# Six block copies per head batch, from ScalarE instructions to DMA transfers inside SBUF, in a chunked RWKV-7 and gated-MLP trunk

## The chip, the core and the metric

The kernel runs on one core of a Trainium2 chip (trn2). The metric is the device time of one launch in microseconds; lower is better. A core has TensorE (PE: matmuls, with weight loads shown apart as PEld), VectorE (DVE), ScalarE (ACT), GpSimd (POOL) and SyncE (SP), each with its own instruction queue worked off in order, and 16 DMA engines that carry out the transfers which SP and ACT issue.

## The reference, cut to what matters

The input is 256 tokens of width 2048 in float32. Layer 0 is a bidirectional RWKV-7 mixer of 64 heads of width 64, layer 1 a chunked gated MLP; a final norm closes it. Only layer 0 is touched here:

```
z = h @ w_in                              # 2048 -> r, k, v, gate of 4096 each, and low-rank columns
per head, in both directions, token by token:
  S_t = S_{t-1} diag(w_t) + (S_{t-1} a_t) b_t^T + v_t k_t^T ;   y_t = S_t r_t
out = (group_norm(y) + bonus) * silu(gate) @ w_out
```

The kernel does not step through tokens. It cuts the 256 tokens into 4 chunks of 64 and solves the inner dependence of a chunk with the inverse of a 64x64 unit triangular matrix, for each head, direction and chunk.

## The kernel before

**Batches.** Layer 0 is worked off in 16 batches of 4 heads (256 channels). A batch has 2 directions, 2 tiles of 128 channels, 4 chunks and 2 heads a tile, so 32 triangular matrices. Half h = 0 or 1 (a head of the tile) sits in partitions h*64 to h*64+63, and 16 matrices lie behind each other in the free dimension (index u). `plan` and the loop at the end of the mixer run several batches at once, each one step behind the next: in period p, `mains` projects k and r for batch p and v and gate for batch p-1, `before(p-1)` makes the gram matrices and their inverses, and `after(p-2)` runs the chunk chain. A batch takes about 77 us.

**The weight feed.** All projections are matmuls against weights that stream from HBM. `convert` loads a tile of 128x1024 values into `raw` (SP issues it, L145; L143 for the small low-rank weights `raw_wu`), ACT rounds it into `whi` (L150), DVE makes the rest `wlo` (L151), and PE takes three matmuls of 256 columns from each 128x128 block (L165, L166, L167). There are two `raw` buffers and three pairs of `whi`/`wlo`; a load waits for the `wlo` of the load two before it. A batch takes 16 such tiles (k, r, v, g: four each) and one `raw_wu`. After the last batch the feed turns to `raw_o`, the weights of the output projection.

**The inverse.** `grams` writes the masked gram matrices of a batch into Gs (DVE, L589). `inverses` inverts each 64x64 matrix by 32x32 blocks: the diagonal blocks go into Dt (four ACT copies, L623), DVE transposes Dt (La, L627), runs 62 small steps (L637, L639) and transposes the result into TD and Tn (L642, L643). The lower left block of Gs goes into NQ (L624). PE multiplies NQ with Tn into qp (L651), ACT copies that to the other rows of NQ (L653), PE multiplies with TD (L657), and ACT puts the product into TTs (L660) beside the two diagonal blocks taken from TD (L661, L662). TTs has one buffer for all batches.

**The chain.** For each of the 4 chunks `chain` runs xp (L713), Xs (ACT, L718), uu with TTs (L722), SUV (ACT, L724), then the next state sp (L729) and the outputs yp (L716, L731), and SUV again from the state (ACT, L741). `values` writes transposed v into SUV (ACT, L680) and issues four transfers inside SBUF on SP: two from AR into the part of Gs that `inverses` has read (Gs<-AR, L684), two into RC (RC<-AR, L684). The first pair waits until Dt and NQ have been read, the second until the previous batch's yp has read RC.

**What sets the order.** Each `yield` gives a due time inside the period, and the generators are drained by due time. From that stream the compiler's scheduler makes one fixed order for each engine; a kernel with other instructions gets another order everywhere in the mixer. An engine never passes an instruction that waits.

Of the kernel before, what the change touches and what calls it, by code (L numbers as in the profile page):

```python
# [22 lines left out]
def trunk(tc, x, norm_g, final_norm_g, w_in, mu_prev, mu_next, w0, w_up, a0, a_up, k_k, k_a, r_k,  # L23
          ln_w, ln_b, w_out, g_w_in, g_ln_g, g_ln_b, g_w_s, g_b_s, g_w_out, out):
    nc = tc.nc
    V, S, G, PE = nc.vector, nc.scalar, nc.gpsimd, nc.tensor
# [33 lines left out]
    def sm(name, tag="pg", bufs=2):  # L60
        return psm.tile([P, 512], F32, tag=tag, name=name, bufs=bufs)
# [280 lines left out]
    TTs = c2.tile([P, 2, 16, C], F32, name="TTs")  # L342
# [268 lines left out]
    def inverses(b, f):  # L611

        Gs, AR = f["Gs"], f["AR"]

        def lane(name):
            return se.tile([P, 16 * 33], F32, tag="ln", name=f"{name}{b}", bufs=3)

        Dt = lane("Dt")[:, :512].rearrange("p (t u) -> p t u", u=16)
        NQ = sc.tile([P, 16, 32], F32, tag="vy", name=f"NQ{b}", bufs=2)
        for h in range(2):  # L620
            for q in range(2):
                r0 = h * 64 + q * 32
                S.copy(Dt[r0:r0 + 32].rearrange("p t u -> p u t"), Gs[q * 32:q * 32 + 32, h, :, q * 32:q * 32 + 32])  # L623
            S.copy(NQ[h * 64:h * 64 + 32], Gs[0:32, h, :, 32:64])  # L624
        yield TSUB[0]
        La = se.tile([P, 32, 32], F32, tag="La", name=f"La{b}")
        V.transpose(La, Dt.unsqueeze(2).to_broadcast([P, 32, 2, 16]))  # L627
        xs = lane("X")
        G.memset(xs[:, :512], 0.0)
        G.tensor_scalar(xs.rearrange("p (m r) -> p m r", r=33)[:, :, 0:32:16], diag, 1.0, None, ALU.mult)  # L630
        X = xs[:, :512].rearrange("p (s t) -> p s t", t=16)
        TD = lane("TD")[:, :512]
        for j in range(31, 0, -1):
            yield TSUB[1] - (TSUB[1] - TSUB[0] - 2) * j / 31
            m, n = j // 2, 16 - j // 2
            tv = TD[:, :j * n].rearrange("p (s t) -> p s t", t=n)
            V.tensor_tensor(tv, La[:, j, 0:j].unsqueeze(2).to_broadcast([P, j, n]),  # L637
                            X[:, j:j + 1, m:].to_broadcast([P, j, n]), ALU.mult)
            V.tensor_tensor(X[:, 0:j, m:], X[:, 0:j, m:], tv, ALU.add)  # L639
        yield TSUB[1]  # L640
        Tn = lane("Tn")[:, :512]
        V.transpose(TD.rearrange("p (u t h) -> p t h u", t=16, h=2), X.rearrange("p s t -> p t s"))  # L642
        V.transpose(Tn, TD)  # L643
        TD, Tn = [t.rearrange("p (u t) -> p u t", t=32) for t in (TD, Tn)]
        qp = sm(f"qp{b}", "pq", 1).rearrange("p (u t) -> p u t", t=32)
        R0 = [slice(h * 64, h * 64 + 32) for h in range(2)]
        R1 = [slice(h * 64 + 32, h * 64 + 64) for h in range(2)]
        yield TQ[0]
        for u in range(16):
            for h in range(2):  # L650
                PE.matmul(qp[R1[h], u], NQ[R0[h], u], Tn[R0[h], u], start=True, stop=True)  # L651
        for h in range(2):
            S.copy(NQ[R1[h]], qp[R1[h]])  # L653
        yield TQ[1]
        for u in range(16):
            for h in range(2):
                PE.matmul(qp[R0[h], u], NQ[R1[h], u], TD[R1[h], u], start=True, stop=True)  # L657
        yield TQ[1] + 2
        for h in range(2):
            S.copy(TTs[R0[h], h, :, 32:64], qp[R0[h]])  # L660
            S.copy(TTs[R0[h], h, :, 0:32], TD[R0[h]])  # L661
            S.copy(TTs[R1[h], h, :, 32:64], TD[R1[h]])  # L662

    def values(b, f):

# [121 lines left out]
    def before(b, f):  # L787
        yield from grams(b, f, 1)
        yield from inverses(b, f)
# [340 lines left out]
    for tt in range(TT):  # L1130
        rstd2 = rms(total(part2[:, tt:tt + 1], f"ssq2_{tt}", hp), f"rstd2_{tt}", hp, V)
        for m in range(NM):
            h = h1[m][:, tt]
# [37 lines left out]
```

## Time and profile before

| what | value |
|---|---|
| median of 3 runs | 2230.92 us (2229.87 to 2234.58) |
| the profiled execution | 2229.16 us, span 2227.4 us |
| granted TensorE clock | 0.995 |
| busy: PE, PEld, DVE, ACT, POOL | 2179.0, 1944.7, 1608.1, 1345.2, 171.8 us |
| mixer batches, by their inverses | first Dt copy at 105.6 us, last at 1254.6 us |
| output projection with the feed alone | from about 1262 to 1445 us |
| gated MLP, its projections and the final norm | from about 1445 us on |

The busy time of an engine is the union of its instructions. A PE interval overlaps the next one, since matmuls are pipelined: in the rows of the timeline a 256-column matmul lasts 0.28 us but the next starts 0.12 us after it. A wait in the table of waits is idle time of an engine, put down to what ended last before it went on.

### The profile page before, as it was taken

To read this page: it belongs to the slowest core of one execution; us is meant where nothing else is said; L and a number is where in the kernel's file an instruction comes from. 1 tells how busy PE (TensorE), PEld (TensorE's weight loads), DVE (VectorE), ACT (ScalarE), POOL (GpSimd) and SP (SyncE) were. 2 spreads that over 40 slices of the span, in tenths; PEclk is the share of its full clock that TensorE was granted. 3 is DMA by queue.
4 is the path that set the end of the run, shared out by engine and by line. 5 is a ranking of instruction groups with operands and counts; after the bars stand their busy time and mean duration, and the time that the engine had idled before them with its cause. 6 is when DMAs were issued, how large, how long until landed. Compare 5 with 4: busy or idle time off the path is not lost.

```text
span 2227.4 us, 48630 instructions
## 1 busy us (share of the span) xinstructions
PE 2179.0 (98%) x19984; PEld 1944.7 (87%) x19984; DVE 1608.1 (72%) x3121; ACT 1345.2 (60%) x2128; POOL 171.8 (8%) x230
## 2 busy tenths in 40 slices
PE   7999999999999999999999999999999999999998
PEld 7889999999999999999999877778888888888886
DVE  5797788787977977887888764465546777777444
ACT  6556777777767676776767664464444444444443
POOL 2210110011001101100010000000000000000000
PEclk9999999999999999999999999999999999999999
DMA  5555444454445544444545555586766666665664
GB/s 167 140 145 142 109 126 134 125 137 112 130 127 143 139 126 131 129 125 136 137 124 138 167 174 177 173 263 189 221 204 190 198 189 195 195 193 192 195 198 154
DMA packets 352687, 356.01 MB, mean 160 GB/s; under 512 B 78160, under 2 KB 300112, under 8 KB 352336
## 3 DMA queue, kind: packets, MB, share of 16 engines
q1 hardware_dynamic: 332208, 331.66, 51.6%
q10 hardware_dynamic: 20256, 21.24, 3.2%
q8 instruction: 157, 2.57, 0.5%
q14 instruction: 66, 0.54, 0.1%
HBM read 329.78 MB, written 6.29 MB: 151 GB/s over the span
## 4 chain that ended last, share of the span: by engine, by line
PE 69%; ACT 10%; DMA 9%; DVE 8%; issue 3%; ACTq 0%; SPq 0%; POOL 0%; POOLq 0%; DVEq 0%
PE uacc L204 5%; PE gacc L204 5%; DMA raw_o<-in_rwkv_w_out_dram 3%; PE oacc L166 3%; PE oacc L167 3%; PE oacc L165 3%; PE gp L584 3%; PE gacc L206 3%; PE uacc L206 3%; PE vacc L167 3%; PE vacc L165 3%; PE vacc L166 3%; ACT Dt L623 2%; PE accv L165 2%; PE accg L167 2%
## 5 line engine op out<-in xcount | busy, mean ns | idle before, releaser
L204 PE MATMUL uacc<-z,whi_u 128*128 128x512 f32 x512 | 179.0, 394 | 0.0
L204 PE MATMUL gacc<-z,whi_g 128*128 128x512 f32 x512 | 177.3, 393 | 0.0
L167 PE MATMUL accg<-zh,wlo_wg 128*128 128x256 f32 x512 | 149.6, 292 | 2.5 <-DVE wlo_wg L151 2.4
L165 PE MATMUL accv<-zh,whi_wv 128*128 128x256 f32 x512 | 149.2, 291 | 1.1 <-ACT whi_wv L150 1.1
L167 PE MATMUL accr<-zh,wlo_wr 128*128 128x256 f32 x512 | 148.7, 290 | 0.6 <-DVE wlo_wr L151 0.5
L165 PE MATMUL acck<-zh,whi_wk 128*128 128x256 f32 x512 | 148.1, 289 | 1.1 <-ACT whi_wk L150 1.1
L165 PE MATMUL accr<-zh,whi_wr 128*128 128x256 f32 x512 | 149.0, 291 | 0.0
L165 PE MATMUL accg<-zh,whi_wg 128*128 128x256 f32 x512 | 148.4, 290 | 0.0
L166 PE MATMUL accr<-zl,whi_wr 128*128 128x256 f32 x512 | 148.1, 289 | 0.0
L167 PE MATMUL accv<-zh,wlo_wv 128*128 128x256 f32 x512 | 147.5, 288 | 0.1
L167 PE MATMUL acck<-zh,wlo_wk 128*128 128x256 f32 x512 | 146.2, 286 | 1.0 <-DVE wlo_wk L151 1.0
L166 PE MATMUL accv<-zl,whi_wv 128*128 128x256 f32 x512 | 147.2, 287 | 0.0
L166 PE MATMUL accg<-zl,whi_wg 128*128 128x256 f32 x512 | 147.0, 287 | 0.0
L166 PE MATMUL acck<-zl,whi_wk 128*128 128x256 f32 x512 | 147.0, 287 | 0.0
L206 PE MATMUL uacc<-z,wlo_u 128*128 128x256 f32 x512 | 142.4, 284 | 0.0
L206 PE MATMUL gacc<-z,wlo_g 128*128 128x256 f32 x512 | 140.2, 279 | 0.0
L151 DVE TENSOR_TENSOR wlo_v<-raw_v,whi_v 128x1024 fp32r<-128x1024 f32 x64 | 78.4, 1225 | 80.4 <-ACT whi_v L150 80.4
L151 DVE TENSOR_TENSOR wlo_o<-raw_o,whi_o 128x1024 fp32r<-128x1024 f32 x64 | 78.2, 1224 | 77.5 <-ACT whi_o L150 77.2
L639 DVE TENSOR_TENSOR X<-X,TD 128x126 f32<-128x126 f32 (+22 forms) x496 | 126.5, 255 | 9.4
L637 DVE TENSOR_TENSOR TD<-La,X 128x126 f32<-128x126 f32 (+22 forms) x496 | 125.6, 253 | 10.6
L151 DVE TENSOR_TENSOR wlo_p<-raw_p,whi_p 128x1024 fp32r<-128x1024 f32 x60 | 73.9, 1232 | 75.7 <-ACT whi_p L150 75.7
L150 ACT CAST whi_p<-raw_p 128x1024 fp32r<-128x1024 f32 x60 | 63.1, 1051 | 91.5 <-PE oacc L167 87.3
(331 smaller groups left out, 6842.3 us busy)
## 6 DMA issues: line engine op xcount, KB each, us to landing
raw_wk<-in_rwkv_w_in_dram SPq DMA_DIRECT2D x64, 512.0 KB, 3.7
raw_wr<-in_rwkv_w_in_dram SPq DMA_DIRECT2D x64, 512.0 KB, 3.7
raw_wv<-in_rwkv_w_in_dram SPq DMA_DIRECT2D x64, 512.0 KB, 3.7
raw_wg<-in_rwkv_w_in_dram SPq DMA_DIRECT2D x64, 512.0 KB, 3.7
raw_o<-in_rwkv_w_out_dram SPq DMA_DIRECT2D x64, 512.0 KB, 4.0
raw_v<-in_gmlp_w_in_dram SPq DMA_DIRECT2D x64, 512.0 KB, 3.7
raw_u<-in_gmlp_w_in_dram SPq DMA_DIRECT2D x64, 512.0 KB, 3.5
raw_g<-in_gmlp_w_in_dram SPq DMA_DIRECT2D x64, 512.0 KB, 3.6
```

What stands on the lines that cost most here:

```text
L150: latest[0] = S.copy(hi, raw)
L151: latest[1] = V.tensor_tensor(lo, raw, hi.bitcast(F32), ALU.subtract)
L165: PE.matmul(acc, a[0], b[0], start=first, stop=False, skip_group_check=True)
L166: PE.matmul(acc, a[0], b[1], start=False, stop=False, skip_group_check=True)
L167: PE.matmul(acc, a[1], b[0], start=False, stop=last, skip_group_check=True)
L204: PE.matmul(acc.rearrange("p h t -> p (h t)"), hi[:, j, cs], zc[:, k].rearrange("p h t -> p (h t)"), start=k == 0, stop=False, skip_group_ ...
L206: PE.matmul(acc[:, 0], lo[:, j, cs], zc[:, k, 0], start=False, stop=k == KT - 1, skip_group_check=True)
L584: PE.matmul(gp[h][:, c].rearrange("p q t -> p (q t)"), BK[H[h], d, cl, c].rearrange("p q t -> p (q t)"), AR[H[h], d, cl, c].rearrange("p q ...
L623: S.copy(Dt[r0:r0 + 32].rearrange("p t u -> p u t"), Gs[q * 32:q * 32 + 32, h, :, q * 32:q * 32 + 32])
L637: V.tensor_tensor(tv, La[:, j, 0:j].unsqueeze(2).to_broadcast([P, j, n]), X[:, j:j + 1, m:].to_broadcast([P, j, n]), ALU.mult)
L639: V.tensor_tensor(X[:, 0:j, m:], X[:, 0:j, m:], tv, ALU.add)
```

## The change

Three of the four kinds of block copies in `inverses` leave ACT. The copy of the lower left block of Gs into NQ (two a batch) and those of the diagonal blocks of TD into TTs (four a batch) become DMA transfers that SP issues. Each moves 32 partitions x 16 x 32 values, 64 KB in runs of 128 bytes. The TTs transfers are also written earlier in the source, ahead of the due time `TQ[1] + 2`. The Dt copies and those out of PSUM (L653, L660) stay on ACT. Lines behind the first edit keep their numbers up to L657; then the new transfers are L659 and L660, and old lines from L658 stand one higher from there on (L684 becomes L685, L722 becomes L723), the copy of qp into TTs becomes L663.

```diff
@@ inverses
             for q in range(2):
                 r0 = h * 64 + q * 32
                 S.copy(Dt[r0:r0 + 32].rearrange("p t u -> p u t"), Gs[q * 32:q * 32 + 32, h, :, q * 32:q * 32 + 32])
-            S.copy(NQ[h * 64:h * 64 + 32], Gs[0:32, h, :, 32:64])
+            nc.sync.dma_start(NQ[h * 64:h * 64 + 32], Gs[0:32, h, :, 32:64])
...
         for u in range(16):
             for h in range(2):
                 PE.matmul(qp[R0[h], u], NQ[R1[h], u], TD[R1[h], u], start=True, stop=True)
+        for h in range(2):
+            nc.sync.dma_start(TTs[R0[h], h, :, 0:32], TD[R0[h]])
+            nc.sync.dma_start(TTs[R1[h], h, :, 32:64], TD[R1[h]])
         yield TQ[1] + 2
         for h in range(2):
             S.copy(TTs[R0[h], h, :, 32:64], qp[R0[h]])
-            S.copy(TTs[R0[h], h, :, 0:32], TD[R0[h]])
-            S.copy(TTs[R1[h], h, :, 32:64], TD[R1[h]])
```

The order moves in three places that matter below; a digit behind a name is the batch. First SP's queue where batch 9's gram matrices are done (about 782 to 795 us before). Before:

```order
L145 DMA raw_wr10_0_10767<-in_rwkv_w_in_dram 128x4x256
L145 DMA raw_wr10_4_10826<-in_rwkv_w_in_dram 128x4x256
L145 DMA raw_wr10_8_10904<-in_rwkv_w_in_dram 128x4x256
L684 DMA Gs9_10428<-AR9_10072 64x16x64 x2
L145 DMA raw_wr10_12_10965<-in_rwkv_w_in_dram 128x4x256
```

SP's queue at the same place now:

```order
L145 DMA raw_wr10_0_10767<-in_rwkv_w_in_dram 128x4x256
L145 DMA raw_wr10_4_10826<-in_rwkv_w_in_dram 128x4x256
L624 DMA NQ9_10742<-Gs9_10428 32x16x32 x2
L685 DMA Gs9_10428<-AR9_10072 64x16x64 x2
L145 DMA raw_wr10_8_10904<-in_rwkv_w_in_dram 128x4x256
L145 DMA raw_wr10_12_10965<-in_rwkv_w_in_dram 128x4x256
```

The load `raw_wr10_8` has moved from ahead of the transfers inside SBUF to behind them. The Gs transfers overwrite what the NQ transfers read, so they wait for these to land. Then ACT's queue at the same place. Before:

```order
L150 CAST whi_wk10_12_10702<-raw_wk10_12_10700 128x1024
L680 COPY SUV8_10606<-vp8_10608 64x4x128 x4
L150 CAST whi_wr10_0_10769<-raw_wr10_0_10767 128x1024
L623 COPY Dt9_10741<-Gs9_10428 32x16x32 x2
L624 COPY NQ9_10742<-Gs9_10428 32x512
L623 COPY Dt9_10741<-Gs9_10428 32x16x32 x2
L624 COPY NQ9_10742<-Gs9_10428 32x512
L718 COPY Xs8_0_10680<-xp8_0_10671 128x256
L150 CAST whi_wr10_4_10828<-raw_wr10_4_10826 128x1024
```

ACT's queue there now:

```order
L719 COPY Xs8_0_10680<-xp8_0_10671 128x256
L150 CAST whi_wk10_12_10702<-raw_wk10_12_10700 128x1024
L725 COPY SUV8_10606<-uu8_0_10718 64x4x64 x2
L623 COPY Dt9_10741<-Gs9_10428 32x16x32 x4
L150 CAST whi_wr10_0_10769<-raw_wr10_0_10767 128x1024
L742 COPY SUV8_10606<-SJ8_0_10796 64x4x64 x2
L150 CAST whi_wr10_4_10828<-raw_wr10_4_10826 128x1024
```

The four Dt copies now stand together with the NQ copies gone, and the first chunk of batch 8's chain (Xs, SUV) has moved ahead of them. Last, SP's queue where TTs of batch 8 is filled (about 751 to 762 us before). Before:

```order
L145 DMA raw_wg8_0_10229<-in_rwkv_w_in_dram 128x4x256
L684 DMA RC_333<-AR8_8968 64x16x64 x2
L145 DMA raw_wg8_4_10289<-in_rwkv_w_in_dram 128x4x256
L145 DMA raw_wg8_8_10373<-in_rwkv_w_in_dram 128x4x256
L145 DMA raw_wg8_12_10457<-in_rwkv_w_in_dram 128x4x256
```

And now:

```order
L685 DMA RC_333<-AR8_8968 64x16x64
L145 DMA raw_wg8_0_10229<-in_rwkv_w_in_dram 128x4x256
L685 DMA RC_333<-AR8_8968 64x16x64
L145 DMA raw_wg8_4_10289<-in_rwkv_w_in_dram 128x4x256
L145 DMA raw_wg8_8_10373<-in_rwkv_w_in_dram 128x4x256
L659 DMA TTs_331<-TD8_9662 32x16x32
L660 DMA TTs_331<-TD8_9662 32x16x32
L659 DMA TTs_331<-TD8_9662 32x16x32
L660 DMA TTs_331<-TD8_9662 32x16x32
L145 DMA raw_wg8_12_10457<-in_rwkv_w_in_dram 128x4x256
```

The four TTs transfers stand ahead of the load `raw_wg8_12`. They wait for batch 8's TD (L642), which DVE's order places right behind the `wlo` of `wg8_0` now and right ahead of that of `wg8_12` before:

```order
L151 TENSOR_TENSOR wlo_wg8_0_10232<-raw_wg8_0_10229,whi_wg8_0_10231 128x1024
L755 BN_STATS st6_7_10302<-yp7_9559 128x6 x3
L642 STREAM_TRANSPOSE TD8_9662<-X8_9659 128x32x16
L755 BN_STATS st6_7_10302<-yp7_9559 128x6
L756 BN_AGGR mv7_10303<-st6_7_10302 128x2
```

The 62 small steps of the inverse have thus moved forward by about three weight tiles against the feed.

## The prediction, made before the changed kernel had run

> **What bounds the kernel now.** I read the page's busy times first, then the windows by stage, then the waits of PE, then the timeline around one batch's inverse.
>
> ```profile
> span 2227.4 us, 48630 instructions
> PE 2179.0 (98%) x19984; PEld 1944.7 (87%) x19984; DVE 1608.1 (72%) x3121; ACT 1345.2 (60%) x2128; POOL 171.8 (8%) x230
> ...
> 80.00:240.00 160.00, 150.47 (x1618) 142.25 (x1617) 131.13 (x271) 98.79 (x155) 22.21 (x25) 0.96 0.51 137
> 240.00:880.00 640.00, 636.61 (x7823) 590.60 (x7822) 525.93 (x1238) 460.81 (x800) 69.34 (x85) 1.00 0.48 128
> 880.00:1262.00 382.00, 377.04 (x4679) 353.04 (x4678) 317.65 (x745) 275.63 (x476) 34.78 (x49) 1.00 0.50 134
> 1262.00:1445.00 183.00, 177.44 (x1405) 139.74 (x1405) 97.94 (x176) 91.18 (x140) 4.96 (x5) 0.99 0.55 175
> ```
>
> The columns of a window are busy us of PE, PEld, DVE, ACT and POOL, then clock, DMA share and GB/s. In the mixer PE is the bound: it idles 160.00 - 150.47 = 9.5 us while the first batches fill, 3.4 us in the eight batches from 240 to 880 us, 5.0 us from there to 1262, and 5.6 us in the output projection, 23.5 us together. ACT, the engine that the change relieves, is busy 460.81 of 640 us. So most of what ACT saves is not on the path. What can be won is idle time of PE that ends on ACT, and what PE's own new order is worth. The idle time of PE from 80 to 1310 us, the rows that carry the argument:
>
> ```profile
> PE yp L731 <- ACT SUV L724: 2.8, 4, 1.1
> PE accg L167 <- DVE wlo_wg L151: 2.4, 1, 2.4
> ...
> PE vp L673 <- ACT TTs L660: 1.3, 2, 0.9
> ...
> PE accv L165 <- ACT whi_wv L150: 1.1, 1, 1.1
> PE qp L657 <- ACT NQ L653: 1.1, 1, 1.1
> ...
> PE xp L713 <- ACT SUV L680: 0.7, 3, 0.3
> PE accr L167 <- DVE wlo_wr L151: 0.5, 1, 0.5
> ```
>
> Each row has total us, times, longest. The two rows on wlo say that PE has hardly ever waited for a projection weight: once for a gate tile, once for an r tile, in all 16 batches. The feed runs ahead of PE.
>
> **Part 1, what leaves ACT.** The copies, with minimum, median and maximum ns:
>
> ```profile
> L624 ACT COPY NQ<-Gs x32: 615/618/622, 107.8 to 1255.7; 32x512 f32<-32x512 f32 x32
> ...
> L661 ACT COPY TTs<-TD x32: 602/617/622, 171.9 to 1301.2; 32x512 f32<-32x512 f32 x32
> L662 ACT COPY TTs<-TD x32: 613/616/624, 172.5 to 1301.8; 32x512 f32<-32x512 f32 x32
> ```
>
> 96 copies of about 0.617 us are 59.2 us, 3.7 us a batch, and ACT should fall from 1345 to about 1286 us. Beside the 77 us that a batch takes nearly all of that is hidden already. On the path lie the places where a chain copy that PE waits for stands behind the removed ones in ACT's queue. One of them:
>
> ```profile
> 1023.64 2.18 ACT L623 COPY Dt<-Gs 32x512 f32<-32x512 f32 x2
> 1025.85 0.62 ACT L624 COPY NQ<-Gs 32x512 f32<-32x512 f32 x1
> 1026.48 0.76 ACT L724 COPY SUV<-uu 64x256 f32<-64x256 f32 x2
> ...
> 1026.90 0.33 PE L731 MATMUL yp<-SUV,Gs 128*64 128x64 f32 x2 [1.00 <-ACT SUV L724]
> ```
>
> PE lost 1.00 us waiting for a SUV copy that stood behind two NQ copies, 1.24 us. The five rows of waits on ACT above (SUV twice, TTs, whi_wv, NQ) add up to 7.0 us, and all but about 0.4 us of them begin within about seven us of removed copies. I credit **-6.6 us**. Bounds: 0, if the new order puts other instructions there, and -13 us as an estimate, about twice these rows, if the remaining small waits of PE on ACT go too.
>
> **Part 2, PE's new order.** PE executes the same matmuls. Counted in the two orders, it passes from one kind of work to another (weights, grams, chain, inverse) 3222 times before and 3163 times now. What such a passage costs is in the timeline:
>
> ```profile
> 701.07 0.28 PE L166 MATMUL acck<-zl,whi_wk 128*128 128x256 f32 x1
> 701.19 0.28 PE L167 MATMUL acck<-zh,wlo_wk 128*128 128x256 f32 x1
> 701.40 0.49 PE L584 MATMUL gp<-AR,BK 64*128 64x128 f32 x4
> ...
> 703.65 0.39 PE L165 MATMUL acck<-zh,whi_wk 128*128 128x256 f32 x1
> 703.88 0.28 PE L166 MATMUL acck<-zl,whi_wk 128*128 128x256 f32 x1
> ```
>
> A weight matmul follows another after 0.12 us; the step into the gram takes 0.21 us and the first one behind it 0.23 us, so about 0.1 us is lost at each passage. 59 passages less are **-5 us**, with ends of 0 (kinds differ in price) and -6.
>
> **Part 3, what SP and the DMA engines get.** Each batch adds six issues and 6 x 512 runs of 128 bytes. The trace has no such transfer. The nearest rows are the transfers inside SBUF that are there, in runs of 256 bytes, beside a weight load:
>
> ```profile
> raw_wr<-in_rwkv_w_in_dram SPq DMA_DIRECT2D x64, 512.0 KB, 3.7
> RC<-AR SPq DMA_DIRECT2D x32, 256.0 KB, 5.2
> Gs<-AR SPq DMA_DIRECT2D x32, 256.0 KB, 3.7
> ...
> L684 SPq DMA_DIRECT2D Gs<-AR x32: 590/596/665, 108.5 to 1256.3; - x32
> ...
> DMA to landing us min/median/max: 3.4/4.1/7.5
> ```
>
> An issue of 1024 runs costs SP 0.60 us; one of 512 runs should cost between that of a weight load, 0.37 us (below), and 0.60, so six cost 2.2 to 3.6 us of SP's 77. SP mostly waits. A landing takes 3.4 to 7.5 us; I take 3.7, since the pieces are smaller.
>
> Where can that reach PE? At batch 9 the load of wr10_8 now stands behind two NQ and two Gs transfers. Before:
>
> ```profile
> 783.95 1.29 DVE L589 TENSOR_TENSOR Gs<-gp,gmask 128x512 f32<-128x512 f32 x2 [1.57 <-PE gp L584]
> 787.59 0.37 SPq L145 DMA_DIRECT2D raw_wr<-in_rwkv_w_in_dram  x1
> 789.07 3.43 SPq L684 DMA_DIRECT2D Gs<-AR  x2
> 792.17 2.00 ACT L150 CAST whi_wr<-raw_wr 128x1024 fp32r<-128x1024 f32 x2
> 794.74 1.21 DVE L151 TENSOR_TENSOR wlo_wr<-raw_wr,whi_wr 128x1024 fp32r<-128x1024 f32 x1
> 800.15 0.28 PE L167 MATMUL accr<-zh,wlo_wr 128*128 128x256 f32 x1
> ```
>
> The load was issued at 787.59 and landed at about 791.3; its cast, the second of the two, began about 793.1, its wlo ended at 795.95, and PE used that first at 800.15. So its cover is 1.8 us ahead of the cast and 4.2 us behind wlo, 6.0 us. Now NQ can be issued when Gs is done, 785.24, twice 0.4 us; it lands by 789.7. The second Gs transfer waits for the fourth Dt copy, at about 786.2 + 4 x 1.09 = 790.6, and is issued by 791.2, then the load: 3.7 us later than before. Queueing behind small runs may add 1.5 us, which is what RC's 5.2 us stands above Gs's 3.7. That is 5.2 of 6.0 us: covered, with little left. Gs itself frees no later, since the wait for two NQ copies in ACT's queue is replaced by a landing that runs beside the Dt copies. At TTs four issues, 1.6 us, and their runs, up to about 2.8 us as an estimate (twice the 1.5 us above, rounded down), stand ahead of one gate tile a batch. TD is not late there: DVE makes it three tiles earlier than before, and the previous batch's uu must only have read TTs, which RC's transfer two places ahead needs of yp as well. I cost part 3 at **+2.5 us**: about 2 us in the output projection, where the last TTs transfers stand in a feed that is itself the bound (PEld is busy only 139.74 of 183 us there), and 0.5 us for the first batches, whose tiles come just in time. Ends: 0 and +27 us (below).
>
> **The sum.** 2229.2 us (the profiled execution; span 2227.4) - 6.6 - 5 + 2.5 = 2220.1 us. The median of the runs lies 1.8 us above that execution, so **2222 us**. Here 0.2%, 4.5 us, is about what a measurement can tell from no change.
>
> **Rival A: hidden, no change.** What ACT gives up is replaced by other waits of the same size. For it: PE idles only 3.4 us in eight batches, and the five rows come from a few chance meetings in the queues. Against it: the copies were really ahead of what PE waited for. Time: the median, about 2230 us, give or take 4.
>
> **Rival B: slower, the feed comes late behind the SBUF transfers.** 13 of the 16 batches have both Gs transfers between NQ and the next weight load. The load leaves SP at 785.24 + 0.8 + landing + 0.6 once that is later than 791.2; with the 1.5 us of queueing the cover of 6.0 us is used up at a landing of 5.4 us, and from there each further us is lost by PE. At 7.5 us, the largest of the rows, that is 2.1 us in each of 13 batches, +27 us; midway, 1.05 us and +14 us: 2230.9 + 14 = **2245 us**. For it: the runs are half as long as the 256-byte ones, whose 256 KB already take as long as 512 KB of weights. The Trainium skill points the same way: its page "DMA: Bandwidth & Descriptors", section "Issuing engines are not separate DMA queues", says that transfers of all issuers share the 16 DMA engines and interleave, and its section "Specifications" sets 512 bytes as the least run for full rate. By that section the longer landing would be the rule. The same page's section "Why small descriptors are slow (HBM only)" says the opposite for transfers inside SBUF, and by it this rival falls away. The trace sides with the first for 256-byte runs, which move half the bytes a microsecond of a weight load, and shows no 128. Against it: the DMA share there is 0.48, and PE waited for wlo twice in all.
>
> **Rival C: the chain gains more.** The new order has the inverse three tiles earlier and the chain's first copies ahead of Dt, so PE's later small waits go as well: -13 - 6 + 1 = -18, 2213 us. For it: 5.0 us of idle time from 880 to 1262 us. Against it: DVE, busy 525.93 of 640 us, sets these places too.
>
> **Chances.** My forecast (2217 to 2226) 0.42, rival C (2207 to 2217) 0.13, rival A 0.25, rival B 0.20. Faster by over 0.2%: forecast and C without their edges, 0.53; within 0.2%: 0.27; slower: 0.20. The range takes the forecast, A and most of C, and the mild end of B: 2209 to 2240.
>
> **What would show it.** ACT busy near 1286 us and 96 copies fewer; the wait of yp on SUV below 1 us in total; no new row of PE on wlo_wr or wlo_wg above 1 us; NQ landings of 3 to 4.5 us; SP's Gs<-AR waits on ACT Dt, not on NQ. It is wrong if PE waits on wlo_wr in many batches, if SP stands at TTs until TD is done, or if the PE waits on ACT only change places.

## The result, and the profile after

The changed kernel takes 2212.7 us (2208.5 to 2216.2, 4 runs) against 2232.5 us before beside it: ratio 0.991, 95% interval 0.989 to 0.994, about 20 us faster. The profiled execution took 2209.9 us. Its page, first the span and the busy times:

```profile
span 2208.1 us, 48735 instructions
PE 2169.0 (98%) x19984; PEld 1938.5 (88%) x19984; DVE 1611.7 (73%) x3121; ACT 1289.0 (58%) x2032; POOL 160.7 (7%) x230
```

ACT has 96 instructions and 56.2 us less. The span fell by 19.3 us: PE's idle time (span less busy) from 48.4 to 39.1 us, its busy time from 2179.0 to 2169.0. The same 19984 matmuls therefore take 10.0 us less even where PE does not wait. By stage (busy us of PE, PEld, DVE, ACT and POOL, then clock, DMA share, GB/s; the third stage ends, and the fourth begins, 12 us earlier than in the table of before):

```profile
80.00:240.00 160.00, 155.07 (x1638) 147.91 (x1637) 133.79 (x263) 95.26 (x149) 23.15 (x26) 0.95 0.53 140
240.00:880.00 640.00, 636.43 (x7953) 591.48 (x7952) 534.74 (x1275) 432.48 (x755) 64.08 (x86) 1.00 0.52 136
880.00:1250.00 370.00, 367.77 (x4627) 344.50 (x4626) 311.20 (x722) 256.15 (x441) 29.79 (x49) 1.00 0.55 143
1250.00:1430.00 180.00, 176.48 (x1336) 139.14 (x1335) 99.12 (x173) 89.34 (x134) 5.38 (x5) 1.00 0.59 181
```

From 240 to 880 us PE is as busy as before (636.4 and 636.6), but gets through 7953 matmuls instead of 7823. The waits of PE from 80 to 1310 us, the largest first:

```profile
PE accg L167 <- DVE wlo_wg L151: 2.8, 2, 2.4
PE gp L584 <- DVE Gs L589: 1.7, 1, 1.7
PE yp L732 <- ACT SUV L725: 1.4, 2, 0.8
PE xp L714 <- ACT SUV L681: 1.3, 1, 1.3
PE qp L657 <- ACT NQ L653: 0.9, 1, 0.9
PE oacc L165 <- ACT whi_o L150: 0.8, 2, 0.6
PE vp L674 <- ACT TTs L663: 0.7, 1, 0.7
...
PE uu L723 <- DMA Gs<-AR: 0.5, 1, 0.5
```

All rows of this view, with those left out here, sum to 11.9 us, against 21.1 us before. No r tile was waited for, and the new transfers show up at most in the 0.5 us of uu on Gs<-AR, which stands behind the NQ transfers in SP's queue.

Where the time went is seen at one place in the timeline, batch 12's gram matrices and batch 11's chain. After:

```profile
1004.40 0.69 PE L723 MATMUL uu<-Xs,TTs 128*64 128x64 f32 x16
1005.13 0.74 ACT L725 COPY SUV<-uu 64x256 f32<-64x256 f32 x2 [1.08 <-PE uu L723]
1006.21 1.29 DVE L589 TENSOR_TENSOR Gs<-gp,gmask 128x512 f32<-128x512 f32 x2 [0.90 <-PE gp L584]
1006.93 1.26 SPq L624 DMA_DIRECT2D NQ<-Gs  x2
1006.93 4.33 ACT L623 COPY Dt<-Gs 32x512 f32<-32x512 f32 x4 [1.06 <-DVE Gs L589]
1008.45 0.69 PE L730 MATMUL sp<-SUV,BT 128*64 128x64 f32 x16
1008.96 0.64 PE L732 MATMUL yp<-SUV,Gs 128*64 128x64 f32 x16
1010.12 1.80 SPq L685 DMA_DIRECT2D Gs<-AR  x2
```

Before, the rows that stand ahead of those shown in part 1:

```profile
1019.99 0.69 PE L722 MATMUL uu<-Xs,TTs 128*64 128x64 f32 x16
1020.79 2.20 ACT L623 COPY Dt<-Gs 32x512 f32<-32x512 f32 x2
1023.00 0.62 ACT L624 COPY NQ<-Gs 32x512 f32<-32x512 f32 x1
...
1023.65 3.44 SPq L684 DMA_DIRECT2D Gs<-AR  x2
```

In both, uu is done when Dt begins. Before, its copy into SUV had to wait for all six copies and started 5.7 us after the first of them; now it stands ahead of Dt and starts 1.8 us before it. The next two steps, sp and yp, then run while ACT does Dt, each in one block of 16. Before, PE lost 1.00 us in front of yp and began it with a piece of two. The groups of the chain's output in the table by line (count | busy us, mean ns | idle), before and after:

```profile
L731 PE MATMUL yp<-SUV,Gs 128*64 128x64 f32 x1024 | 59.4, 226 | 2.9 <-ACT SUV L724 2.8
L716 PE MATMUL yp<-SUV,RC 128*64 128x64 f32 x768 | 41.5, 222 | 0.0
```

```profile
L732 PE MATMUL yp<-SUV,Gs 128*64 128x64 f32 x1024 | 53.6, 225 | 1.4 <-ACT SUV L725 1.4
L717 PE MATMUL yp<-SUV,RC 128*64 128x64 f32 x768 | 37.2, 222 | 0.0
```

One matmul lasts as long as ever, but more of them overlap. Counted from start to start and without the waits, so that nothing counts twice, the steps of yp took 76.3 us before and 70.4 after. Of the unbroken groups of yp, 20 ran as one block of 16 before, and 49 do now.

That place is not one of its kind. Over batches 1 to 15, the SUV copy of the previous batch's first chunk starts ahead of Dt in 2 batches before, and in 9 after. In batches 9 to 15 it starts 8.2 us behind the first Dt copy before, and from then on 5.7 and some 16 us behind it in turn; after, from batch 8 on, 1.8 to 2.0 us ahead of it in every one. The gain follows that: the first matmul on v weights of batch 5 starts at 496.3 us before and 497.1 after, that of batch 14 at 1200.1 and 1185.6, so 1.7 us a batch (15.3 us over nine). The output projection and what is left of the last chains give the rest, and from the gated MLP on (1495.3 and 1475.5 us) the distance stays the same to within 0.5 us.

### The profile page after: what moved, and what is told of

Same layout as the page of the kernel before. It is cut to its first block, busy times and chain, and to the rows that moved or that the text cites. A ratio compares the mean times of both kernels' runs of the same rounds, so it can differ in the third digit from the quotient of the medians.

```text
span 2208.1 us, 48735 instructions
## 1 busy us (share of the span) xinstructions
PE 2169.0 (98%) x19984; PEld 1938.5 (88%) x19984; DVE 1611.7 (73%) x3121; ACT 1289.0 (58%) x2032; POOL 160.7 (7%) x230
## 4 chain that ended last, share of the span: by engine, by line
PE 77%; DMA 8%; DVE 7%; ACT 6%; issue 2%; POOL 0%; SPq 0%; ACTq 0%; POOLq 0%; DVEq 0%
PE uacc L204 5%; PE gacc L204 5%; DMA raw_o<-in_rwkv_w_out_dram 3%; PE gp L584 3%; PE oacc L166 3%; PE oacc L167 3%; PE oacc L165 3%; PE uacc L206 3%; PE gacc L206 3%; PE vacc L165 3%; PE vacc L166 3%; PE vacc L167 3%; PE accg L167 2%; PE accv L167 2%; PE accv L165 2%; PE accv L166 2%
```

## The experiments

Theory P: what counts is ACT's time at one place, between Gs and the chain's copies and casts, and of the removed copies only those of NQ stood there. Its main rival is O, that every kernel gets another order, which alone is worth some us either way. T and D belong to single runs. These are the letters from run 5 on. The first four expectations were written before P had this form: their R is wider, relief wherever PE waits on ACT, and gave each half of the change about 9 us.

All runs in one table: time, ratio to the kernel before measured beside it, batches out of 15 in which that first SUV copy starts ahead of Dt, PE's idle time (span less busy) and granted clock of the profiled execution. The kernel before runs at 2229 to 2233 us beside them, with 2 batches, 48.4 us idle, clock 0.995. Where a few us matter, runs that were not measured beside each other are compared below by their distance from it.

| kernel | us | ratio, 95% interval | SUV ahead | PE idle | clock |
|---|---|---|---|---|---|
| the change | 2212.7 | 0.991 (0.989 to 0.994) | 9 | 39.1 | 0.994 |
| 1 NQ alone by DMA | 2211.3 | 0.992 (0.990 to 0.993) | 10 | 42.2 | 0.996 |
| 2 TTs alone by DMA | 2228.5 | 0.999 (0.998 to 1.000) | 2 | 49.7 | 0.997 |
| 3 the change and six idle ACT copies | 2220.7 | 0.996 (0.994 to 0.997) | 8 | 42.8 | 0.995 |
| 4 TTs copies earlier, on ACT | 2229.8 | 1.000 (0.999 to 1.001) | 2 | 45.9 | 0.994 |
| 5 NQ by DMA and idle ACT copies in its place | 2222.6 | 0.997 (0.996 to 0.998) | 0 | 51.8 | 0.994 |
| 6 NQ alone by GpSimd | 2210.8 | 0.991 (0.990 to 0.993) | 10 | 37.8 | 0.995 |
| 7 before, another due time | 2234.7 | 1.002 (1.001 to 1.003) | 2 | 50.7 | 0.996 |
| 8 the change, another due time | 2209.0 | 0.990 (0.989 to 0.992) | 9 | 42.4 | 0.996 |
| 9 before, NQ copied twice | 2238.6 | 1.004 (1.003 to 1.006) | 0 | 50.6 | 0.991 |
| 10 NQ by DMA, Dt by GpSimd | 2231.4 | 1.001 (1.000 to 1.002) | 0 | 44.2 | 0.991 |
| 11 NQ by DMA, half of Dt by GpSimd | 2220.2 | 0.996 (0.994 to 0.997) | 2 | 41.3 | 0.994 |
| 12 all six copies by GpSimd | 2222.6 | 0.996 (0.994 to 0.997) | 7 | 42.1 | 0.992 |

**Each half alone.** Run 1 is the first edit alone:

```diff
-            S.copy(NQ[h * 64:h * 64 + 32], Gs[0:32, h, :, 32:64])
+            nc.sync.dma_start(NQ[h * 64:h * 64 + 32], Gs[0:32, h, :, 32:64])
```

> Only the NQ copies (two a batch) go by DMA; the four TTs copies stay on ACT as before. Theory R (relief: what counts is ACT time taken away ahead of what PE waits for): NQ stands right behind Dt in ACT's queue, ahead of the chain's SUV and of the next casts, so it carries the larger part of the PE waits that went, about -9 of the -20 us although it is a third of the ACT time: 2223 us. Theory O (order: any other stream of instructions gives another order, and this one happens to be good): no relation to the share; anything from 2215 to 2240.

Run 2 is the second alone, and takes 64 of the 96 copies off ACT:

```diff
+        for h in range(2):
+            nc.sync.dma_start(TTs[R0[h], h, :, 0:32], TD[R0[h]])
+            nc.sync.dma_start(TTs[R1[h], h, :, 32:64], TD[R1[h]])
         yield TQ[1] + 2
...
-            S.copy(TTs[R0[h], h, :, 0:32], TD[R0[h]])
-            S.copy(TTs[R1[h], h, :, 32:64], TD[R1[h]])
```

> Only the TTs copies (four a batch) go by DMA, issued early in the source as in the changed kernel; NQ stays on ACT. Theory R: two thirds of the ACT time, but mostly where ACT has slack: about -9 us, 2223 us, and the two parts add up to about -20. Theory O: the two parts do not add up; anything from 2215 to 2240. If four transfers behind each other ahead of a gate tile cost something, it shows here: PE would wait on wlo_wg in more than two places.

The busy times, of NQ alone and then of TTs alone:

```profile
PE 2166.8 (98%) x19984; PEld 1934.4 (88%) x19984; DVE 1611.9 (73%) x3121; ACT 1327.6 (60%) x2096; POOL 158.4 (7%) x230
```

```profile
PE 2177.0 (98%) x19984; PEld 1942.0 (87%) x19984; DVE 1605.8 (72%) x3121; ACT 1306.0 (59%) x2064; POOL 178.7 (8%) x230
```

NQ alone gives the whole gain with 17.6 us off ACT; TTs alone gives none that can be told from zero, with 39.2 us off. So ACT's total time is not what counts, and R is out in its wider form too: it gave 2223 us for each half. Run 1 is faster than both theories allowed (O began at 2215 us), and run 2 lies inside the wide range of O.

**Idle ACT copies.** Run 3 adds six copies a batch, which nobody reads, to the changed kernel:

```diff
+            S.copy(dumo[0:32], smask[0:32, 1:2].to_broadcast([32, 512]))
...
+            for q in range(2):
+                S.copy(dumo[0:32], smask[0:32, 1:2].to_broadcast([32, 512]))
```

> The changed kernel with six copies a batch put back on ACT at the old places in the source, of the same size (32 partitions x 512 values) from a constant into a scratch tile that nobody reads: ACT has the old work, the data still goes by DMA. Theory R: ACT's time is what counted, so the gain goes, 2226 to 2233 us. Theory O, or a theory that data comes earlier by DMA: the gain stays in large part, 2210 to 2218 us.

At 2220.7 us it falls between the two ranges, and it does not test what it was meant to. Copies that depend on nothing were placed early in the program: ACT is busy 62.4 us of the first 80, 49.9 in the changed kernel, and from 240 to 880 us as little as there.

```profile
0.00:80.00 80.00, 63.24 (x491) 61.43 (x492) 44.72 (x86) 62.39 (x112) 14.12 (x43) 1.00 0.56 163
240.00:880.00 640.00, 636.87 (x7904) 591.28 (x7904) 529.09 (x1255) 431.87 (x751) 63.46 (x85) 1.00 0.52 136
```

Run 4 leaves the TTs copies on ACT, but writes them where run 2 writes its transfers:

```diff
+        for h in range(2):
+            S.copy(TTs[R0[h], h, :, 0:32], TD[R0[h]])
+            S.copy(TTs[R1[h], h, :, 32:64], TD[R1[h]])
         yield TQ[1] + 2
```

> The kernel before, with the four TTs copies from TD still on ACT but written two due steps earlier, where the changed kernel issues its transfers; NQ as before. No DMA is added and ACT has all its old work. Theory R: no gain, 2228 to 2236 us. Theory O: a good part of the gain may come from the place in the source: 2215 to 2225 us.

No change, as R gave: the earlier place in the source does nothing here, and by run 2 the engine of the TTs copies does not matter either.

**The place itself.** Run 5 moves NQ to DMA and lets ACT copy the same block into a scratch tile. These copies depend on Gs, and in ACT's queue they stand where the NQ copies stood:

```diff
-            S.copy(NQ[h * 64:h * 64 + 32], Gs[0:32, h, :, 32:64])
+            nc.sync.dma_start(NQ[h * 64:h * 64 + 32], Gs[0:32, h, :, 32:64])
+            S.copy(dumo[h * 64:h * 64 + 32], Gs[0:32, h, :, 32:64])
```

> NQ comes by DMA, and ACT still copies the same block of Gs into a scratch tile that nobody reads. The two copies stand in ACT's queue where the NQ copies stood, between and behind the four Dt copies; the TTs copies are on ACT as before. Theory P (what counts is ACT's 1.24 us a batch at that very place, ahead of the chain's copies and the casts): the gain of NQ by DMA alone, 18.5 us, is lost again, 2225 to 2234 us. Rival T (NQ has to be ready earlier, or Gs has to be free earlier, and ACT's queue is not what counts): the gain stays, 2209 to 2215. Rival O (any other order of the engines is worth some us either way): anything from 2205 to 2235, and then the passages of PE (mixer, profile) go with the time, not the copies.

11.8 of the 18.5 us are lost again, and no batch has SUV ahead of Dt any more. P had expected all of it to go; 2222.6 us lies below its range and above that of T. The place in its timeline, batch 12:

```profile
1014.54 1.31 SPq L625 DMA_DIRECT2D NQ<-Gs  x2
1014.54 2.18 ACT L624 COPY Dt<-Gs 32x512 f32<-32x512 f32 x2 [1.07 <-DVE Gs L590]
1015.12 0.60 PE L675 MATMUL vp<-ident,Vt 128*128 128x128 f32 x4
1016.74 0.62 ACT L626 COPY dumo<-Gs 32x512 f32<-32x512 f32 x1
1017.38 2.17 ACT L624 COPY Dt<-Gs 32x512 f32<-32x512 f32 x2
...
1019.57 0.62 ACT L626 COPY dumo<-Gs 32x512 f32<-32x512 f32 x1
...
1021.29 2.37 ACT L682 COPY SUV<-vp 64x512 f32<-64x512 f32 x4
...
1021.97 0.45 PE L715 MATMUL xp<-SUV,Gs 128*64 128x64 f32 x8
```

Batch 11's chain has not begun when Dt starts: vp runs beside it and xp only after it, where the changed kernel had uu behind it already. In the batches next to it, 11 and 13, SUV starts 5.7 us behind the first Dt copy, so the two forms take turns as they do in the kernel before. Idle copies at this place thus undo most of the gain, though nothing waits for their result; T predicted that it would stay. The 6.7 us that remain are near the size of what another order does (run 7).

Run 6 takes NQ to GpSimd instead of DMA; the orders of PE and ACT are nearly those of run 1:

```diff
-            S.copy(NQ[h * 64:h * 64 + 32], Gs[0:32, h, :, 32:64])
+            G.tensor_copy(NQ[h * 64:h * 64 + 32], Gs[0:32, h, :, 32:64])
```

> The NQ copies alone leave ACT, for GpSimd and not for DMA; the orders of PE and ACT are nearly those of the kernel with only NQ by DMA (2211.3 us). Theory P: the same gain, since ACT is relieved at the same place: 2207 to 2214 us, the lower if the six issues and the 128-byte runs cost the feed something, the higher if GpSimd's copy is slow. Rival D (it is the DMA path itself that helps): 2225 to 2232. Rival O: with the same orders the same time as with NQ by DMA, 2209 to 2214.

The same time as by DMA, so D is out: what helps is that the NQ copies leave ACT, and not where they go. The NQ transfers cost nothing that can be measured (a gain of 18.4 us by DMA, 18.5 by GpSimd).

**Another order.** Runs 7 and 8 change one due time, in the kernel before and in the changed one:

```diff
-(8.0, 44.0), (59.05, 66.0), 66.05
+(8.0, 40.0), (59.05, 66.0), 66.05
```

> The kernel before with one due time changed: the inverse's small steps are spread to 40 instead of 44 of the period. All copies stay on ACT. It is a measure of what another order alone does. Theory P: within 6 us of before, 2224 to 2236 us. Rival O: it may fall as far as the changed kernel, 2212 to 2222.

> The changed kernel with the same due time changed, 40 instead of 44: another order, the copies still by DMA. Theory P: the gain stays, 2208 to 2219 us. Rival O: the gain came with the one order of the changed kernel, and goes back towards 2222 to 2232.

The kernel before moved by +5.3 us. The changed one is 20.4 us below the kernel before beside it, where the change itself was 19.8 below its own, so it moved by 0.6; the distance between the two is 25.7 us here. So this other order was worth up to some 5 us, and the gain did not hang on the last detail of one order. It is a mild test: the column "SUV ahead" did not move, 2 and 9, so it says nothing of an order with another form.

**Doses.** Run 9 copies NQ a second time on ACT, into scratch:

```diff
             S.copy(NQ[h * 64:h * 64 + 32], Gs[0:32, h, :, 32:64])
+            S.copy(dumo[h * 64:h * 64 + 32], Gs[0:32, h, :, 32:64])
```

> The kernel before, in which ACT also copies each NQ block a second time into a scratch tile that nobody reads, right behind the NQ copy: 2.48 us instead of 1.24 us a batch among the four Dt copies. Theory P: the place costs about 11 us for each 1.24 us a batch there, by the two kernels with NQ by DMA with and without the idle copy (2222.6 and 2211.3 us), so 2236 to 2250. Rival O (the order alone): within the 6 us that another due time did, 2224 to 2236. Rival T (the readiness of NQ or Gs): Gs is free 1.24 us later a batch for the transfer that overwrites it, NQ no later, 2227 to 2234.

9.2 us slower, in the lower part of what P gave. Part of that is the clock: the median run of this kernel was granted 0.9935, of the kernel before 0.995, and 0.0015 of 2230 us is 3.3 us. The 5.9 us that are left are near the 5.3 us of run 7, so this run does not decide between P and O.

Runs 10 and 11 go the other way. NQ comes by DMA, and the Dt copies go to GpSimd, all four or every second:

```diff
-                S.copy(Dt[r0:r0 + 32].rearrange("p t u -> p u t"), ...)
+                G.tensor_copy(Dt[r0:r0 + 32].rearrange("p t u -> p u t"), ...)
```

> NQ by DMA and the four Dt copies a batch by GpSimd, so ACT has nothing left at that place, 4.36 us a batch less than with NQ by DMA alone (2211.3 us); the TTs copies are on ACT as before. Theory P, if the price per us at that place held on: 2175 us or less; but PE idles only about 17 us between 80 and 1430 us there, so what is left is bounded by that and by fewer passages, 2195 to 2208. If the place is used up once the copies of NQ are gone: 2208 to 2216. If GpSimd's strided copies are much slower than 1.1 us, La comes later and the time rises over 2216.

> As the kernel before this one, but only two of the four Dt copies a batch go to GpSimd, and the two engines work beside each other, so La starts earlier too. Theory P: 2.18 us a batch less on ACT at that place, 2198 to 2209 us. If the place is used up: 2208 to 2216. Rival O: anything within 6 us of 2211.

Here P fails, and run 11 lies outside every range that was given for it. ACT is freed of 4.4 or 2.2 us more a batch at the place, and the time goes up by 20.4 and 9.3 us against run 1. GpSimd is not too slow for it, and DVE hardly waits for Dt any more ahead of La (44.3 us before, 27.7 in run 1). The Dt copies of run 10, and who waited for them (us, times):

```profile
L623 POOL COPY Dt<-Gs x64: 1030/1084/2164, 104.6 to 1261.0; 32x512 f32<-32x512 f32 x64
...
  DVE La L627: 3.1, 2
```

What goes with the loss is the order (0 and 2 batches with SUV ahead), and in run 10 the clock. The stretch from 240 to 280 us, and below it the same in the changed kernel:

```profile
240.00:280.00 40.00, 34.10 (x314) 31.23 (x314) 30.82 (x83) 20.92 (x44) 10.96 (x11) 0.74 0.27 64
```

```profile
240.00:280.00 40.00, 39.60 (x421) 36.22 (x420) 32.69 (x81) 29.20 (x55) 5.70 (x8) 1.00 0.46 114
```

314 matmuls instead of 421: by an estimate from the clock, 0.74 costs 0.26 x 40 = 10.4 us there. That is one execution; the median clock of run 10 over its 12 executions is 0.993, against 0.995 in run 1, which is about 4.5 us of the 20.4.

Run 12 does all six copies by GpSimd:

```diff
-            nc.sync.dma_start(NQ[h * 64:h * 64 + 32], Gs[0:32, h, :, 32:64])
+            G.tensor_copy(NQ[h * 64:h * 64 + 32], Gs[0:32, h, :, 32:64])
...
-            nc.sync.dma_start(TTs[R0[h], h, :, 0:32], TD[R0[h]])
-            nc.sync.dma_start(TTs[R1[h], h, :, 32:64], TD[R1[h]])
+            G.tensor_copy(TTs[R0[h], h, :, 0:32], TD[R0[h]])
+            G.tensor_copy(TTs[R1[h], h, :, 32:64], TD[R1[h]])
```

> All six copies a batch by GpSimd instead of by DMA: ACT is relieved as in the changed kernel, no transfer is added, and GpSimd gets 96 copies of about 0.60 us. If the transfers of the changed kernel cost the feed or the tail something (the 2.5 us of the prediction), this is the fastest version: 2205 to 2210 us. If they are hidden: 2208 to 2214, the same as the changed kernel. In either case theory P expects PE's idle time ahead of the gated MLP between 19 and 26 us, as in all kernels without the NQ copies on ACT, and not the 29 to 33 us of those with them. Rival O: 2214 or more.

It is no better version: 2222.6 us, in the range of O. PE's idle time from its first matmul to the gated MLP is 23.7 us by the trace, inside the 19 to 26 that P expected (the kernels with copies in NQ's place on ACT lie at 27.3 to 33.2), but the time is not the one that goes with it. The clock from 240 to 280 us is 0.83, which by the same estimate is 6.8 us; but the change has a stretch of 0.83 too, from 80 to 120 us, so this explains little of the distance between them. And yt now waits for yn:

```profile
240.00:280.00 40.00, 38.90 (x352) 36.02 (x351) 29.75 (x70) 24.13 (x44) 7.61 (x9) 0.83 0.38 100
```

```profile
PE yt L777 <- ACT yn L767: 3.7, 4, 1.8
```

**What the runs leave.** Which copies matter is shown: those of NQ, by leaving ACT at that place, for DMA or for GpSimd alike (runs 1, 2, 5 and 6). One part of P stands besides. PE's idle time is 45.9 to 51.8 us in the six kernels that have two or four more ACT copies among the Dt copies, and 37.8 to 44.2 us in the eight that have none; runs 1 and 5, which differ in these copies, lie at 42.2 and 51.8. The other part, so many us of time for each us of ACT there, does not hold.

What goes with the time is which side of the Dt copies the chain's first SUV copy stands on. With 9 or 10 batches ahead: 2209.0, 2210.8, 2211.3 and 2212.7 us. With 0 to 2: 2220.2 to 2238.6 us. With 7 and 8: 2222.6 and 2220.7. The last two are not better than the best of the second group, but their early batches hide it. From batch 10 to batch 14 a batch (from its first matmul on v weights to that of the next) takes 75.8 to 76.6 us in the six kernels that have SUV ahead in all of these batches, runs 3 and 12 among them, and 77.1 to 79.2 us in the eight that do not. Runs 3 and 12 were 9.5 and 8.8 us behind the change when batch 10 began.

PE's busy time is lowest in the four kernels with 9 or 10 batches ahead, 2164.8 to 2170.8 us against 2173.2 to 2191.6. Where only NQ left ACT, or NQ and TTs by DMA, the scheduler's order settled into the form with SUV ahead from batch 6 or 8 on; with copies on ACT at that place it never did. That the form is the cause is not shown: no run turns it alone, with all else as it was. It was not tried, and it would need an order written by hand. No run beat the change clearly.

## Why the prediction was right or wrong, point by point

**The outcome.** 2212.7 us lies in the range of 2209 to 2240 and on the side that was given the largest chance, but outside the forecast's own 2217 to 2226. The gain was twice the forecast, so it was the width of the range that held, and not the sum. Rival C's 2213 was the time that came, in part by luck: of C's terms, -13 for idle time measured -9.3, and -6 for PE's order measured -10.0, and the two errors cancel. C also named the mechanism that the runs left standing, the chain's first copies ahead of Dt, and gave it 0.13.

**Part 1, inside its bounds for a wrong reason.** PE's idle time fell by 9.3 us where -6.6 was credited. But the five rows of waits behind the removed copies fell only from 7.0 to 4.3 us: yp on SUV from 2.8 to 1.4, vp on TTs from 1.3 to 0.7, accv on whi_wv from 1.1 to nothing, qp on NQ from 1.1 to 0.9, while xp on SUV rose from 0.7 to 1.3. The rest of the gain lay in rows that were not quoted. The largest of them, before, is gone after:

```profile
PE uu L722 <- ACT Xs L718: 2.4, 6, 0.6
```

The step that failed was to price the removed copies by their neighbours in the queue, and to treat all six alike: run 2 shows that the four TTs copies were worth nothing.

**Part 2, the right sign at half the size.** 59 passages fewer at 0.1 us are 5.9 us, of which 5 were taken; PE's busy time fell by 10.0. The counts of 3222 and 3163 stand in no view of a trace. Whether the price or the count was too small depends on what is counted. In the traces PE turns from one written tile to another (by name, so acck, gp, xp and so on) 1641 times before, 1523 after and 1548 in run 1. That is 118 fewer after, about 0.085 us each. But in run 1 it is 93 fewer, and its PE is 12.2 us less busy, so no single price a passage fits both. Most of the saving sits in yp, whose steps fell by 5.9 us, as more of its groups now run unbroken; the next largest fall, in qp and bp, is about 2 us each.

**Part 3, too dear.** +2.5 us was taken, and the runs put it near 0. With the four TTs transfers a batch the gain is 19.8 us (the change), without them 18.4 (run 1); with the NQ transfers it is 18.4 (run 1), with GpSimd in their place 18.5 (run 6). The 2 us put on the output projection did not come: PE idled 5.6 us in that window before and 3.5 after. The issue was dearer than the 0.4 us taken, the landing shorter than the 3.7 us:

```profile
L624 SPq DMA_DIRECT2D NQ<-Gs x32: 591/592/1356, 107.5 to 1237.9; - x32
...
DMA to landing us min/median/max: 2.1/2.7/5.1
```

The condition of rival B, a landing over 5.4 us, was met by none of the 32 (the TTs transfers reached 6.1). The rate of the short runs is another matter. By the packet records of the trace a packet of 128 bytes took 13 ns in the median, one of 256 bytes 22 ns and one of 1024 bytes, a weight load's, 46 ns: 10, 12 and 22 bytes a ns. Here the trace sides with the section "Specifications" of the Trainium skill's page "DMA: Bandwidth & Descriptors", which sets 512 bytes as the least run for full rate, and not with its section "Why small descriptors are slow (HBM only)", which exempts transfers inside SBUF. The lower rate cost nothing that can be measured, since a transfer has only 512 packets: spread evenly over 16 engines they are 0.4 us, as an estimate, of a landing of 2.7.

**What was to show it.** ACT near 1286 us (1289.0) and 96 copies fewer: both seen. No new row on wlo_wr or wlo_wg over 1 us: right, that of wlo_wg went from 2.4 to 2.8. The wait of yp on SUV below 1 us: wrong, 1.4. NQ landings of 3 to 4.5 us: wrong, 2.7 in the median. SP standing at TTs until TD is done, which was to be a sign of being wrong, came 7 times, 5.3 us at the longest; no wait of PE on it shows. SP's Gs<-AR transfers waiting for Dt and not for NQ: wrong, they waited for NQ's landing 18 times:

```profile
SPq L685 <- DMA NQ<-Gs: 29.5, 18, 3.4
```

It did no harm. In the timeline above Gs<-AR leaves 3.2 us behind the first Dt copy, and left 2.9 us behind it before. Rival A's objection, that the five rows come from chance meetings in the queues, was nearly right about the rows. It did not save the rival, since what came with the new order was worth more than they were.

## What to carry to other kernels

Where a scheduler makes one fixed order, compare the two orders on which side of the longest run of work on an engine the first copy of a chain that repeats stands, batch by batch; a copy taken from that place can go with a whole chain moving ahead by a step, and here 17.6 us off ACT there gave 18.4 us, while 39.2 us off elsewhere gave none. Don't price PE's order by one count of passages at one price. Run a control that changes the order and nothing else: here a due time moved the kernel by 5.3 us, so smaller effects of an edit can't be told from its order. Compare the time a batch takes once the order has settled, too; the total can hide it behind a bad start.

## What the runs showed of the hardware

- What a DMA issue costs SP follows neither the bytes nor the number of runs alone: 512 runs of 128 bytes inside SBUF cost 0.592 us, 1024 runs of 256 bytes inside SBUF 0.596, and a weight load from HBM, 512 runs of 1024 bytes, 0.37.
- Short DMA runs moved fewer bytes a ns: a packet of 128 bytes took 13 ns in the median, of 256 bytes 22, of 1024 bytes 46 (the trace of the change).
- GpSimd copied a 32x512 block as fast as ACT: 0.602 us (run 6) against 0.618 (before) for NQ, 1.084 (run 10) against 1.084 (before) for the strided Dt. Where it had the TTs copies too (run 12), these took 0.87 and 0.98 us in the median.
- The granted clock fell for stretches in every kernel, mostly between 40 and 200 us (0.91 from 80 to 120 us before, 0.83 in the change). In runs 10, 12 and 11, which use GpSimd for Dt or TTs, it also fell to 0.74, 0.83 and 0.91 from 240 to 280 us, where it stayed at 1.00 before, in the change and in runs 1 and 9. In each of the three the clock records fall to half 0.7 to 2.6 us behind a wait of PE of 0.7 to 1.9 us; in the kernel before, 1.1 us behind one of 1.7 us. That the wait is the cause is not shown: one of 2.4 us in the kernel before, ending at 135 us, was followed by none.
